# Log-sum-exp per head: batch 6's results are finished at the end of the kernel instead of at tiles 57 and 58

## The chip, the cores and the metric

The kernel runs on one core of a Trainium2 chip. Five engines work beside each other, each through its own list of instructions in order: TensorE (PE; its weight loads are listed as PEld), VectorE (DVE), ScalarE (ACT), GpSimd (POOL) and SyncE (SP), which here issues DMAs. A DMA can also be issued from ACT's list. The metric is the time on the device of one execution, in microseconds (us). Three timed runs of the kernel before gave 322.15, 322.24 and 322.38; the median is 322.24.

## The reference

The input x has 8 batches of 2048 rows of 2048 float32 numbers. Each row is cut into 8 heads of 256, and each head has a bias of 256 numbers.

```python
x_heads = x.reshape(B, S, H, Dh).transpose(0, 2, 1, 3)
x_heads = x_heads + bias[None, :, None, :]
x_tiled = np.repeat(x_heads, 2, axis=2)
mx = x_tiled.max(axis=-1, keepdims=True)
lse = mx.squeeze(-1) + np.log(np.exp(x_tiled - mx).sum(axis=-1))
```

So for each batch, head and row the output is the logarithm of the sum of exp(x + bias) over the head's 256 numbers, written twice in succession. The output has the shape 8 x 8 x 4096.

## The kernel before

A tile is 256 rows: 128 partitions with 2 rows (`K = 2`) of 2048 numbers each. There are 64 tiles, 8 to a batch; the program calls the count `T` and numbers the tiles 0 to 63. Eight tile buffers (`xb`) are filled by DMAs from SP. All of x is read once, 134 MB.

The kernel takes no maximum. For each head of each row it needs the sum of exp(x + bias). Some heads have their bias added in PSUM by TensorE (two multiplications, one that lays down the bias and one that adds x through the identity), and ACT takes the exponential and the sum in one instruction (L458 in the last tiles, followed by an instruction that reads the accumulator). For the others ACT takes the exponential of x alone (L483), and DVE multiplies by exp(bias) and sums (L518, `weigh`), or POOL multiplies and folds in halves (L535, L541) and DVE sums the remaining 32 (L548). In most tiles (0 to 53) POOL adds the bias ahead of the exponential (L477) and DVE sums (L502). The sums go to small tiles `R`, one for each group of batches.

The last three tiles, 61 to 63, are not worked on as tiles. The text `TAIL` lists, word by word, which step is put into the program next: an addition in PSUM (`add`, L806), an exponential (`exp`), a sum with bias (`sum`), a weighing, a fold. The rows of these tiles are called e, f, a, b, c and d; "b:0" is head 0 of row b. Their loads are cut into 13 pieces, `TAIL_LOADS`, in the order in which they are wanted; the last three are c:01, b:0 and b:1. The list ends with the sum of b:0 (ACT) and the sum of the folded c:7 (DVE). Both belong to batch 7.

The whole program is in an order written out by hand: each engine runs its instructions in the order in which the program calls them. Waits between engines follow from the tiles that instructions read and write. An instruction that the scheduler would tie to another bank of the same PSUM tile is freed from it by `on_bank`. PSUM has two tiles of two banks each, `pairs`; banks 0 and 1 are the first pair, 2 and 3 the second. A counter, `n_ps`, hands out the banks in turn. It goes up by 1 for each of the tiles 0 to 53, by 2 for each of the tiles 54 to 60 (one for each row), by 1 for each of the 11 words `add`, and by 1 in `turn_two`.

When the sums of some batches are complete they are turned by TensorE, so that rows lie along the free dimension, ACT takes the logarithm and writes each number twice, and a DMA stores the result. There are four such endings:

- two groups of batches 0 to 5, in `finish` (L577), at tiles in the middle, into `res`;
- batch 6, in `turn_two` (L698, two turns of 128 x 64) and `finish_two` (L711, 64 x 512 out), into `res_two`;
- batch 7, in `finish_last` (turn L716, logarithm L722, DMA L723 issued from ACT), into `res_last`, as the last thing.

In the kernel before, `turn_two` is called at the end of tile 57 (`t == T - 7`) and `finish_two` at the end of tile 58. The stores of the first two groups and of batch 6 are all issued in `store`, which is called ahead of the list of the last tiles. On SP they stand behind the last loads, in this order: L582 twice, L586 once.

Last of all `judge` looks at the bit patterns of the sums (L607, L626, L633): when an exponential was out of range, a slow second version would compute everything again. Every engine reads this verdict and branches. Then SP waits for every DMA, the stores among them, and the kernel ends.

Of the kernel before, what the change touches and what calls it, by code (L numbers as in the profile page):

```python
# [92 lines left out]
def kernel(  # L93
# [6 lines left out]
    nc = tc.nc  # L100
    P = nc.NUM_PARTITIONS
    B, S, D = x.shape
    H, Dh = bias.shape
    assert D == H * Dh and S % (P * KB) == 0
    NBLK = S // (P * K)
    NB = S // (P * KB)
    TB = KB // K
    T = B * NBLK
# [55 lines left out]
    res_two = sb.tile([H * NBLK, P, K, 2], F32, name="res_two")  # L164
# [12 lines left out]
    def modes_of(t):  # L177
        return [modes for t0, modes in STAGES if t0 <= t][-1]

    def pieces(t):  # L180

        if len(modes_of(t)) == 1:
            return [(0, K, 0, D)]
        return [(k, k + 1, 0, D) for k in range(K)]
# [85 lines left out]
    for set_idx, (_name, funcs) in enumerate(get_activation_tables(nc.m.arch).items()):  # L270
# [9 lines left out]
        out=brow.rearrange("p (h j) -> p h j", h=H), in_=bias.unsqueeze(0)  # L280
# [25 lines left out]
    for i, c in enumerate(range(G0, D, MM)):  # L306
# [10 lines left out]
        out=b_far,  # L317
        in_=brow,
# [5 lines left out]
        out=Rx[0][0:1, 1 + widths[0] :],  # L324
# [11 lines left out]
    def other_factors():  # L336
        nc.scalar.activation(
            out=w_ps[:, W_LATE - W0 :], in_=b_rep[:, W_LATE - G0 : W2 - G0], func=ACT.Exp
        )
        nc.scalar.activation(out=w_sb, in_=b_rep[:, W1 - G0 :], func=ACT.Exp)  # L340
# [7 lines left out]
    def on_bank(i, ins):  # L348
        for j, u in bank_users[i // 2]:
            if j != i and u.ins.engine != ins.ins.engine:  # L350
                tc.declare_no_dep(ins.ins, u.ins, reason="another bank")
        bank_users[i // 2].append((i, ins))
        return ins
# [68 lines left out]
    def late_heads(m, t, got, sums):  # L422


        mms = []
        for h, p in enumerate(got[:-1]):
            mm = nc.tensor.matmul(  # L427
                p,
                lhsT=ident,
                rhs=xts[t % NBUF][:, :, h * Dh : (h + 1) * Dh],  # L430
                start=False,
                stop=True,
            )
            mms.append(on_x(t, mm, [loads[t, 0, 0]]))

        def pe_part():
            for k in range(K):
                act = nc.scalar.activation(  # L438
                    out=xts[t % NBUF][:, k, 0:Dh],
                    in_=got[0][:, k * Dh : (k + 1) * Dh],  # L440
                    func=ACT.Exp,
                    accum_out=sums[:, k, 0:1],
                )
                last_uses[t].append(on_x(t, act, [mms[0]]))
            act = nc.scalar.activation(  # L445
                out=xts[t % NBUF][:, :, Dh : m["pe"] * Dh].rearrange(
                    "p k (h j) -> p h k j", j=Dh
                ),
                in_=got[-1].rearrange("p (h k j) -> p h k j", k=K, j=Dh),
                func=ACT.Exp,  # L450
            )
            on_x(t, act, [mms[-1]])

        return pe_part
# [124 lines left out]
    def store():  # L579

        for (b0, b1), r in zip(groups, res):
            nc.sync.dma_start(  # L582
                out=out[b0:b1].rearrange("b h (n r) -> (b h n) r", n=NB),
                in_=r.rearrange("q p k r -> q (p k r)"),
            )
        nc.sync.dma_start(  # L586
            out=out[B - 2].rearrange("h (n r) -> (h n) r", n=NBLK),
            in_=res_two.rearrange("q p k r -> q (p k r)"),
        )

    def ends_of(i):

# [100 lines left out]
    def turn_two():  # L693
        bank = n_ps[0] % len(ps)
        n_ps[0] += 1
        two_in.append(bank)
        for k in range(K):
            turn = nc.tensor.transpose(  # L698
                out=ps[bank][0 : H * NBLK, k * P : (k + 1) * P],
                in_=R[B - 2][:, k].rearrange("p h n -> p (h n)"),  # L700
                identity=ident,
            )
            on_bank(bank, turn)

    def finish_two():
        (bank,) = two_in
        two = ps[bank][0 : H * NBLK]
        tv = bass.AP(
            tensor=two.tensor, offset=two.offset, ap=[two.ap[0], [1, P], [P, K], [0, 2]]
        )  # L710
        on_bank(bank, nc.scalar.activation(out=res_two, in_=tv, func=ACT.Ln))  # L711

    def finish_last():
        bank = n_ps[0] % len(ps)
        last = ps[bank][:, 0:P]
        nc.tensor.transpose(  # L716
            out=last, in_=R_last.rearrange("p h n k -> p (h n k)"), identity=ident
        )
        tv = bass.AP(
            tensor=last.tensor, offset=last.offset, ap=[last.ap[0], [1, P], [0, 2]]  # L720
        )
        nc.scalar.activation(out=res_last, in_=tv, func=ACT.Ln)  # L722
        nc.scalar.dma_start(  # L723
            out=out[B - 1].rearrange("h (n r) -> (h n) r", r=2 * P),
            in_=res_last.rearrange("q p r -> q (p r)"),
        )


    def sums_of(t):

        b, blk = divmod(t, NBLK)
        if b < B - 2:
            return R[b][:, blk % TB * K :, :, blk // TB]
        if b == B - 2:
            return R[b][:, :, :, blk]
        return R_last[:, :, blk, :].rearrange("p h k -> p k h")
# [107 lines left out]
    for t in range(T_TAIL):  # L844
        if t == T_FACTORS:
            other_factors()
        xt = xts[t % NBUF]
        sums = sums_of(t)
        for k0, k1, c0, c1 in pieces(t):
            m = modes_of(t)[k0]  # L850
            add = None
            heads = []
            bias_here = bias_there
            if m["late"]:
                pe_part = late_heads(m, t, bias_here, sums)
                if t == BLOCKS - TB - 1:
                    keep_warm()
            else:
                heads = add_x(m, t, k0, c0, c1, bias_here)

                pe_parts = [
                    lambda t=t, one=one, sums=sums: sum_biased(t, *one, sums)
                    for one in heads
                ]

                def pe_part(pe_parts=pe_parts):
                    flush(pe_parts)

            if not m["late"]:
                if next_units:  # L870
                    bias_there = put_bias(*next_units.pop(0))
            if t > T_PROMPT and m["g0"] == H:
                keep_warm()
            if m["g0"] < H:
                add = g_add(m, t, k0, k1)
            wait_for_pool = t == T_ROWS and k0 == 0
            if not wait_for_pool:
                flush(for_pool)
            h0 = m["pe"]
            h1 = m["g0"]  # L880
            hf = min(h1, H - m["fold"])
            if h0 < h1 and not m["late"]:
                done = exp_inplace(
                    t, xt[:, k0:k1, h0 * Dh : h1 * Dh], loads[t, k0, c0]
                )
                if wait_for_pool:
                    flush(for_pool)
                if hf < h1:
                    for_pool.append(fold(t, k0, hf, h1, sums, [done]))
            flush(for_pe)  # L890
            if not m["late"]:
                for k in range(k0, k1):
                    for h in range(h0, hf):
                        weigh(
                            t,
                            xt[:, k, h * Dh : (h + 1) * Dh],
                            h,
                            sums[:, k, h : h + 1],
                            done,
                        )  # L900

            def pool_part(t=t, m=m, k0=k0, k1=k1, sums=sums, add=add):
                if add:
                    later(m, t, k0, k1, sums, add)
                if k1 == K:
                    reload(t)

            for_pool.append(pool_part)
            if m["g0"] < H:
                pe_part()  # L910
                if t == T_PROMPT - 1:
                    first_factors()
                if m["late"]:
                    bias_there = put_bias(*next_units.pop(0))
                    if t == BLOCKS - TB - 1:
                        keep_warm()
            else:
                for_pe.extend(pe_parts)

        for i, (_, b1) in enumerate(groups):  # L920
            if t - 2 == b1 * NBLK - 1:
                finish(i)
                ends_of(i)
        if t == T - 7:
            turn_two()
        if t == T - 6:
            finish_two()
    store()
    last_bank = heads[0][2]
    to_read[last_bank] = len(for_pe)  # L930
# [6 lines left out]
    for what, row, heads, step in tail:  # L937
# [7 lines left out]
            tail_step(what, *row, heads, step)  # L945
        next_bias()
    assert not for_pe and not for_pool and not to_bias
    finish_last()
    again = judge() > 0

# [33 lines left out]
```

## Time and profile before

| | |
|---|---|
| median of the timed runs | 322.24 us |
| the profiled execution, its own time | 322.7 us |
| its span (first to last instruction) | 320.8 us |
| busy: PE, DVE, ACT, POOL | 77%, 89%, 82%, 90% of the span |
| mean DMA rate | 422 GB/s |
| mean granted TensorE clock | 0.948 |

The profile page gives for each engine its busy time, then groups of instructions by source line ("L711"), and the chain of work that ended last: from the last instruction back to what released it, and so on. A row of a group reads: line, engine, operation, tile written <- tile read, partitions x elements, and the count or the time. A timeline gives the start and the duration of each instruction, and in brackets how long its engine stood idle before it and what it waited for. For a DMA it gives the time that the issuing took; the time to landing, from the issue to the last arrival, stands in the list of DMAs. Times in the views are counted from the start of the span, so the end is at 320.8.

### The profile page before, as it was taken

Reading aid. Unit: us, or ns where it says so; the run is one execution under the profiler, and the core shown is the slowest. Engines: PE = TensorE matmul, PEld = TensorE weight load, DVE = VectorE, ACT = ScalarE, POOL = GpSimd, SP = SyncE. Lnnn points to the kernel's source line nnn. Section 1 sums busy time; section 2 is a strip of 40 time slices with the busy share of each in tenths; the row PEclk is TensorE's granted clock in tenths of the full one; section 3 lists DMA queues with packets and bytes.
Section 4 is the critical chain, followed back from the end, with each engine's and each line's share of the span. In section 5 each row is a group of like instructions: output and inputs, shape, how many; then the busy total and the mean of one; then the engine's idle time right before and its main releaser. Section 6 shows DMA issues by size and latency. Waiting matters only on the chain.

```text
span 320.8 us, 2284 instructions
## 1 busy us (share of the span) xinstructions
PE 248.0 (77%) x619; PEld 100.3 (31%) x619; DVE 286.6 (89%) x303; ACT 263.7 (82%) x437; POOL 287.4 (90%) x116
## 2 busy tenths in 40 slices
PE   5998884977886679868677778877877788597774
PEld 1333332323332224323223323332332332143332
DVE  1337999699989998998999998999999999989996
ACT  1149987698698877879889879888888998999996
POOL 7949997999999999999999999999999999976874
PEclk9989997899799997979999979999999999779998
DMA  7999999999999999999999999999999999999995
GB/s 295 462 421 458 392 459 443 404 453 441 413 453 400 450 447 404 449 441 414 453 410 441 449 402 453 413 435 427 425 435 434 433 425 426 426 428 425 424 413 205
DMA packets 8950, 135.44 MB, mean 422 GB/s; under 512 B 996, under 2 KB 1511, under 8 KB 2791
## 3 DMA queue, kind: packets, MB, share of 16 engines
q1 hardware_dynamic: 8784, 135.14, 98.5%
q10 hardware_dynamic: 152, 0.14, 0.1%
q8 instruction: 5, 0.08, 0.1%
q14 instruction: 9, 0.07, 0.1%
HBM read 134.23 MB, written 1.05 MB: 422 GB/s over the span
## 4 chain that ended last, share of the span: by engine, by line
DMA 42%; DVE 28%; ACT 13%; PE 9%; POOL 6%; issue 0%; SPq 0%
DMA xb<-in_x_dram 42%; DVE R L502 22%; ACT xb L483 10%; POOL xb L477 6%; DVE xb L495 4%; PE pair L427 3%; ACT xb L458 3%; DVE xb L518 2%; PE one_ps L427 2%; PE pair L302 1%; PE pair L369 1%; PE pair L404 1%; DMA brow<-in_bias_dram 1%; ACT xb L445 1%; PE one_ps L369 1%
## 5 line engine op out<-in xcount | busy, mean ns | idle before, releaser
L477 POOL TENSOR_TENSOR xb<-xb,b_rep 128x2048 f32<-128x2048 f32 x57 | 257.6, 4544 | 18.9 <-DMA xb<-in_x_dram 18.9
L502 DVE TENSOR_REDUCE R<-xb 128x14 f32<-128x3584 f32 (+1 forms) x57 | 216.8, 3804 | 3.1 <-ACT xb L483 1.3
L483 ACT ACTIVATE xb<-xb 128x2560 f32<-128x2560 f32 (+8 forms) x79 | 156.7, 1995 | 19.5 <-POOL xb L477 19.5
L427 PE MATMUL pair<-xb,ident 128*128 128x512 f32 x216 | 110.5, 637 | 0.0
L427 PE MATMUL one_ps<-xb,ident 128*128 128x512 f32 x108 | 61.8, 655 | 17.0 <-DMA xb<-in_x_dram 17.0
L445 ACT ACTIVATE xb<-pair 128x1024 f32<-128x1024 f32 x54 | 55.4, 1026 | 17.4 <-PE pair L427 17.1
L427 PEld LDWEIGHTS pair<-xb,ident 128*128 128x128 f32 x216 | 44.3, 205 | 57.8 <-issue 57.8
L495 DVE TENSOR_TENSOR xb<-xb,w_ps 128x512 f32<-128x512 f32 x54 | 36.7, 680 | 20.8 <-ACT xb L483 20.8
L369 PE MATMUL one_ps<-b,ones_bf 128*128 128x512 bf16 x52 | 20.1, 387 | 37.3 <-ACT xb L438 37.3
L438 ACT ACTIVATE xb<-one_ps 128x256 f32<-128x256 f32 x108 | 39.8, 376 | 7.0 <-PE one_ps L427 7.0
L369 PEld LDWEIGHTS <-ones_bf 128*128 128x128 bf16 (+1 forms) x174 | 17.6, 101 | 86.2 <-issue 79.2
L369 PE MATMUL pair<-b,ones_bf 128*128 128x512 bf16 x104 | 30.9, 379 | 0.0
L427 PEld LDWEIGHTS one_ps<-xb,ident 128*128 128x128 f32 x108 | 19.5, 198 | 32.1 <-DMA xb<-in_x_dram 26.2
L518 DVE CUSTOM_DVE_ANT_0 xb<-xb,w_ps 128x256 f32<-128x256 f32 x60 | 22.1, 417 | 0.0
L438 ACT ACTIVATION_READ_ACCUMULATOR xb<-one_ps 128x1 f32 x108 | 22.0, 204 | 0.0
L404 PE MATMUL pair<-xb,ident 128*128 128x512 f32 x28 | 16.6, 698 | 4.9 <-DMA xb<-in_x_dram 4.9
L541 POOL TENSOR_TENSOR xb<-xb 128x128 f32<-128x128 f32 (+3 forms) x36 | 14.0, 388 | 3.3 <-ACT xb L817 0.5
L458 ACT ACTIVATE xb<-pair 128x256 f32<-128x256 f32 x39 | 15.1, 410 | 0.3 <-PE pair L404 0.3
L535 POOL TENSOR_TENSOR xb<-xb,w_sb 128x256 f32<-128x256 f32 (+1 forms) x11 | 9.1, 830 | 4.9 <-ACT xb L483 4.4
L806 PE MATMUL pair<-xb,ident 128*128 128x256 f32 (+1 forms) x22 | 8.1, 456 | 3.4 <-DMA xb<-in_x_dram 3.2
L418 PE MATMUL tp<-b_rep,ident 128*128 128x384 f32 x24 | 9.7, 485 | 0.0
L458 ACT ACTIVATION_READ_ACCUMULATOR xb<-pair 128x1 f32 x39 | 9.3, 238 | 0.0
(59 smaller groups left out, 82.2 us busy)
## 6 DMA issues: line engine op xcount, KB each, us to landing
xb<-in_x_dram SPq DMA_DIRECT2D x20, 4096.0 KB, 21.9
xb<-in_x_dram SPq DMA_DIRECT2D x17, 2048.0 KB, 22.3
xb<-in_x_dram SPq DMA_DIRECT2D x10, 1024.0 KB, 22.3
xb<-in_x_dram SPq DMA_DIRECT2D x2, 640.0 KB, 18.1
xb<-in_x_dram SPq DMA_DIRECT2D x3, 384.0 KB, 12.3
xb<-in_x_dram SPq DMA_DIRECT2D x1, 768.0 KB
xb<-in_x_dram SPq DMA_DIRECT2D x2, 256.0 KB, 15.4
out_dram<-res SPq DMA_DIRECT2D x1, 512.0 KB, 5.8
```

The lines of the kernel that those rows point to most:

```text
L369: nc.tensor.matmul(p, lhsT=lhsT, rhs=each_row(b, h * Dh, Dh, K), start=i == 0, stop=False,)
L404: mm = nc.tensor.matmul(p, lhsT=ident, rhs=xts[t % NBUF][:, ka:kb, c : c + w], start=False, stop=True,)
L427: mm = nc.tensor.matmul(p, lhsT=ident, rhs=xts[t % NBUF][:, :, h * Dh : (h + 1) * Dh], start=False, stop=True,)
L438: act = nc.scalar.activation(out=xts[t % NBUF][:, k, 0:Dh], in_=got[0][:, k * Dh : (k + 1) * Dh], func=ACT.Exp, accum_out=sums[:, k, 0:1],)
L445: act = nc.scalar.activation(out=xts[t % NBUF][:, :, Dh : m["pe"] * Dh].rearrange("p k (h j) -> p h k j", j=Dh), in_=got[-1].rearrange("p ...
L458: act = nc.scalar.activation(out=xts[t % NBUF][:, k, h * Dh : (h + 1) * Dh], in_=p, func=ACT.Exp, accum_out=sums[:, k, h : h + 1],)
L477: add = nc.gpsimd.tensor_tensor(out=v, in0=v, in1=each_row(b_rep, c - G0, D - c, k1 - k0), op=ALU.add)
L483: return on_x(t, nc.scalar.activation(out=v, in_=v, func=ACT.Exp), [after])
L495: mul = nc.vector.tensor_tensor(out=f, in0=f, in1=each_row(w_ps, m["pe"] * Dh - W0, n, k1 - k0), op=ALU.mult,)
L502: red = nc.vector.tensor_reduce(out=sums[:, k0:k1, h0:H], in_=v.rearrange("p k (h j) -> p k h j", j=Dh), op=ALU.add, axis=mybir.AxisListTy ...
L518: ttr = nc.vector.tensor_tensor_reduce(out=v, in0=v, in1=w, scale=1.0, scalar=0.0, op0=ALU.mult, op1=ALU.add, accum_out=dst,)
L541: done = nc.gpsimd.tensor_tensor(out=v[:, :, 0:n], in0=v[:, :, 0:n], in1=v[:, :, n : 2 * n], op=ALU.add)
```

## The change

Batch 6's turn, logarithm and store are all called behind the list of the last tiles, ahead of `finish_last`. TensorE's two turns come behind the addition of b:0, ACT's logarithm behind the sum of b:0. The DMA that stores `res_two` moves from `store` to `finish_two`; it is still SP's third store and last DMA. The bank counter no longer goes up between tiles 57 and 58.

```diff
@@ store
-        nc.sync.dma_start(
-            out=out[B - 2].rearrange("h (n r) -> (h n) r", n=NBLK),
-            in_=res_two.rearrange("q p k r -> q (p k r)"),
-        )
@@ finish_two
         on_bank(bank, nc.scalar.activation(out=res_two, in_=tv, func=ACT.Ln))
+        nc.sync.dma_start(
+            out=out[B - 2].rearrange("h (n r) -> (h n) r", n=NBLK),
+            in_=res_two.rearrange("q p k r -> q (p k r)"),
+        )
@@ the loop over the tiles
-        if t == T - 7:
-            turn_two()
-        if t == T - 6:
-            finish_two()
     store()
@@ behind the list
     assert not for_pe and not for_pool and not to_bias
+    turn_two()
+    finish_two()
     finish_last()
     again = judge() > 0
```

## The prediction

> **What bounds the kernel now.** I read the page first, then busy time by stage, the chain that ended last, ScalarE's own timeline, and the DMA issues. All numbers are microseconds from the span's start unless said otherwise. First the page and the stages of the last 37 us; a stage's row gives its length, busy time of PE, weight loads, DVE, ACT and POOL, granted clock, DMA share and GB/s.
>
> ```profile
> span 320.8 us, 2284 instructions
> core 0: us, PE busy (x) PEld busy (x) DVE busy (x) ACT busy (x) POOL busy (x), PEclk, DMA share, GB/s
> 294.70:305.70 11.00, 8.32 (x25) 3.60 (x24) 10.63 (x66) 11.00 (x27) 8.36 (x20) 1.00 1.01 424
> 305.70:310.70 5.00, 4.23 (x15) 2.06 (x16) 4.91 (x27) 5.00 (x14) 4.04 (x5) 1.00 1.01 414
> 310.70:317.40 6.70, 4.29 (x17) 2.07 (x16) 6.63 (x40) 6.67 (x23) 5.01 (x11) 1.00 0.91 351
> 317.40:320.83 3.43, 0.54 (x4) 0.26 (x4) 0.46 (x2) 0.38 (x1) 0.00 (x0) 0.64 0.13 44
> ```
>
> From 294.7 to 317.4 ScalarE is busy 11.00 of 11.00, 5.00 of 5.00 and 6.67 of 6.70: it has no gap. The DMA engines are full too until the loads run out. So two things run side by side here, and the question is which is ahead. The chain that ended last answers it.
>
> ```profile
> 294.18 0.73 ACT xb L458 x4
> 294.91 0.45 ACT res_two L711
> 295.36 1.37 ACT xb L483
> ...
> 309.79 0.96 ACT xb L483
> 310.74 0.02 issue
> 310.77 0.42 DVE xb L518
> ...
> 317.16 0.10 DVE R L548
> 317.26 0.15 DVE odd L607
> 317.41 0.01 issue
> 317.42 0.33 PE pair L716
> ```
>
> The chain runs on ScalarE and then on VectorE, and batch 6's logarithm (L711) is a link of it. The operation to be moved stands on the path that sets the end. The hand-over to DVE at 310.77 is close: ACT's last sum ends later still, as its timeline shows (columns: start, duration, engine, line, operation, and in brackets idle time before it).
>
> ```profile
> 294.66 0.25 ACT L458 ACTIVATION_READ_ACCUMULATOR xb<-pair 128x1 f32 x1
> 294.75 0.60 ACT L711 ACTIVATE res_two<-pair 64x512 f32<-64x512 f32 x1
> 295.23 1.50 ACT L483 ACTIVATE xb<-xb 128x1536 f32<-128x1536 f32 x1
> ...
> 316.15 0.49 ACT L483 ACTIVATE xb<-xb 128x256 f32<-128x256 f32 x1
> ...
> 316.82 0.46 ACT L458 ACTIVATE xb<-pair 128x256 f32<-128x256 f32 x1
> 317.08 0.29 ACT L458 ACTIVATION_READ_ACCUMULATOR xb<-pair 128x1 f32 x1
> 317.79 0.38 ACT L722 ACTIVATE res_last<-pair 128x256 f32<-128x256 f32 x1 [0.42 <-PE pair L716]
> 318.20 0.39 ACTq L723 DMA_DIRECT2D out_dram<-res_last  x1
> ```
>
> The last sum of the list (b:0) ends at 317.08 + 0.29 = 317.37. Batch 7's turn (L716) starts at 317.42, its logarithm at 317.79, its store at 318.20. DVE's last result is there at 317.26, 0.11 earlier. So ACT is the later of the two by a hair. Behind its last sum ACT stands idle for 0.42 while TensorE turns batch 7.
>
> **The change, part by part.** The sum is made against the profiled execution, 322.7 (a span of 320.8 and 1.9 around it); the median of the three timed runs is 322.24, 0.46 lower, and I carry the difference over to it.
>
> *The logarithm out of tile 58's place.* L711 lasts 0.60, but its successor starts 295.23 - 294.75 = 0.48 behind it, and the chain puts it at 0.45. I take 0.45. No instruction on ACT behind it waits for anything until 317.37, so all of them can start 0.45 earlier if their inputs are there. That needs three covers.
>
> *Cover 1, the loads.* The last loads are issued as those ahead of them land, behind any buffer that ACT still holds. The first two rows are the issue of the load before the last and its time to landing, the third is TensorE's addition of b:0.
>
> ```profile
> L242 SPq DMA_DIRECT2D xb<-in_x_dram x1: 328/328/328, 308.9 to 308.9; - x1
> DMA to landing us min/median/max: 6.3/6.3/6.3
> 315.62 0.60 PE L806 MATMUL pair<-xb,ident 128*128 128x256 f32 x2
> ```
>
> The load before the last is issued at 308.9 and lands at 315.2. The last one (b:1, 128 KB) follows it; at the 424 GB/s of the stage that is 0.31 more, 315.5 (an estimate from these rows). Its exponential starts at 316.15, and would start at 315.70. It still has about 0.2. TensorE adds b:0 in the two multiplications that end at 315.62 + 0.60 = 316.22; its sum starts at 316.82, and would start at 316.37, with 0.15 left. So the loads allow a gain of about 0.45 + 0.15 = 0.6 and no more: the gain is capped just above what I claim.
>
> *Cover 2, DVE.* It must move with ACT, since L716 needs its sums too.
>
> ```profile
> 305.70 0.42 DVE L518 CUSTOM_DVE_ANT_0 xb<-xb,one_ps 128x256 f32<-128x256 f32 x1 [0.38 <-ACT xb L483]
> ```
>
> At 305.70 DVE has been idle for 0.38, waiting for an exponential. At 310.77 the chain hands over from ACT to DVE, so DVE waits for ACT there as well. I count the 0.38 alone: its end goes to 317.26 - 0.38 = 316.88, still before ACT's 317.37 - 0.45 = 316.92, so ACT's 0.45 decides.
>
> *The two turns out of tile 57, into the end.* These are two weight loads and two multiplications on TensorE.
>
> ```profile
> 288.05 0.38 PE L698 MATMUL pair<-ident,R 128*64 128x128 f32 x2
> 317.42 0.33 PE L716 MATMUL pair<-ident,R 128*128 128x128 f32 x1 [1.20 <-DVE odd L607]
> ```
>
> At tile 57 they take 0.38 on an engine that waits for loads there, so removing them gives 0. At the end they are queued behind b:0's addition and ahead of L716. TensorE idles 1.20 before L716, and batch 6's sums were complete many tiles ago, so the 0.38 fits: 0. They need a PSUM bank. Counting the bank counter through the program (68 units of bias, 11 additions), they get bank 3, in the second pair, last read by d:0's sum, which is done before 315.2. Batch 7's turn gets bank 0, in the first pair, as before. So L716 does not wait for batch 6's logarithm. All additions from tile 58's second row on use the bank one lower; the distance between two uses of a bank stays four or grows by one. ACT waits for no addition in that stretch, so that is 0.
>
> *The logarithm into the end.* Queued on ACT behind b:0's sum and ahead of L722. Its place costs 0.48; ACT's free place there is 317.79 - 317.08 less the 0.09 by which L711 starts behind such a read (294.66 to 294.75), that is 0.62. It fits with 0.14 to spare, and moves as a whole with b:0's sum. If the cover were gone, L722 and all behind it would be late by the excess, at most 0.48. I take 0.
>
> *The store.* SP issues it in both kernels as its last DMA, so no load and no store is queued behind it; only SP's read of the verdict and its closing waits are, and the verdict comes later than the issue ends. Before, it was issued early:
>
> ```profile
> 313.05 0.47 SPq L586 DMA_DIRECT2D out_dram<-res_two  x1
> out_dram<-res SPq DMA_DIRECT2D x1, 512.0 KB, 5.8
> out_dram<-res SPq DMA_DIRECT2D x1, 256.0 KB, 5.4
> L582 SPq DMA_DIRECT2D out_dram<-res x2: 343/446/549, 311.1 to 312.1; - x2
> out_dram<-res_two SPq DMA_DIRECT2D x1, 128.0 KB, 4.8
> out_dram<-res_last ACTq DMA_DIRECT2D x1, 128.0 KB, 1.8
> ```
>
> It landed at 317.85, while batch 7's store lands at 318.20 + 1.8 = 320.0 and the span ends 0.8 later. In the new place batch 6's logarithm ends at 316.72 + 0.60 = 317.32 and the store is issued at about 317.35, 0.4 ahead of batch 7's (318.20 - 0.45 = 317.75). The end does not move if it takes less than 317.75 + 1.8 - 317.35 = 2.2. No row shows an SP store into an idle queue. Its bounds are 1.8 (L723, as many bytes, queues empty) and 4.8 (its own row, issued behind 768 KB of stores and the last loads: 512 and 256 KB). The last of those stores lands at 312.1 + 5.4 = 317.5, about when the new issue is made, so hardly anything stands ahead of it. I take 1.8, which costs 0.
>
> [...]
>
> The sum: -0.45 + 0 + 0 + 0 = -0.45. That is 322.25 for a profiled execution and 321.79 for the median, 0.14% less.
>
> **The rivals.** 0.2% is 0.64 us, about what a measurement of this kernel can tell from no change.
>
> 1. *Batch 6's store becomes the last thing to land* (slower). It is exposed where before it had 2 us of cover. At 4.8 it lands at 322.15 instead of batch 7's 320.0 before: +2.15, 324.4. From 2.65 on the change is a loss, from 3.3 on a loss over 0.2%. For it: no row shows the short case on SP. Against it: nothing is left in the queue ahead of it.
> 2. *The loads take the gain.* In the timed runs the loads may land later against ACT than in this execution; 0.6 of later landing eats all of it: 322.24. For it: DMA share 1.01 and only 0.15 to spare. Against it: ACT has no wait in the whole stretch.
> 3. *The end is not covered on ACT or TensorE*: L716 or L722 waits for batch 6's logarithm after all. L716 would start at 317.32 rather than 316.97: +0.35, net -0.10, 322.14. Against it are the banks counted above.
> 4. *The two stores collide.* If batch 7's 128 KB queue wholly behind batch 6's, at 424 GB/s, the end is 0.31 later: net -0.14, 322.1. Against it: the issues are 0.4 apart and each needs 0.31. [...]
> 5. *More than the sum.* If the logarithm's whole 0.60 and the 0.1 or so by which DVE's and TensorE's starts are loosened came back, it would be -0.7, 321.54. Against it: the cap of 0.6 from the loads.
>
> **How the numbers follow.** The forecast (321.79, itself between 321.6 and 321.95) has 0.60; rival 1 has 0.09, rival 2 0.12, rival 3 0.05, rival 4 0.04, rival 5 0.10. Rivals 2, 3 and 4 and the forecast lie within 0.2%. Rival 5 is faster by over 0.2% for the most part, and a little of the forecast's tail with it: 0.13. Rival 1 is slower by over 0.2% for the larger part: 0.08. The rest, 0.79, is no change. The range of 321.45 to 322.55 takes in the forecast, rivals 2 to 5 and the mild end of rival 1, and leaves its 4.8 out.
>
> **What would show it.** In the profile after: an L483 row directly behind the sums of tile 58, with no L711; every ACT start from there on 0.4 to 0.5 earlier; L716 near 316.97; L711's row between b:0's read and L722, with L722's idle time gone or down to about 0.1; a store of 128 KB from SP landing 1.8 to 2.2 after issue. Wrong would be: ACT waiting for a load or an addition behind 295 (rival 2), L716 waiting for res_two's line (rival 3), the SP store at 2.65 or more (rival 1), or L723 above 1.8 (rival 4).

## The result and the profile after

The change made the kernel slower: 323.00 us against 322.28 (medians of 13 runs each), a ratio of 1.0020 with a 95% interval of 1.0011 to 1.0028. That is 0.72 us. The forecast was 0.45 us less than before.

The profiled execution took 322.93, with a span of 321.1. First the end of the list on ScalarE, TensorE and SP after the change, from the timeline (start, duration, engine, line, operation, idle time before it).

```profile
316.36 0.39 ACT L458 ACTIVATE xb<-pair 128x256 f32<-128x256 f32 x1
316.63 0.21 ACT L458 ACTIVATION_READ_ACCUMULATOR xb<-pair 128x1 f32 x1
316.72 0.59 ACT L707 ACTIVATE res_two<-pair 64x512 f32<-64x512 f32 x1
317.26 0.38 ACT L722 ACTIVATE res_last<-pair 128x256 f32<-128x256 f32 x1
317.68 0.39 ACTq L723 DMA_DIRECT2D out_dram<-res_last  x1
...
316.08 0.38 PE L694 MATMUL pair<-ident,R 128*64 128x128 f32 x2
316.90 0.33 PE L716 MATMUL pair<-ident,R 128*128 128x128 f32 x1 [0.43 <-DVE odd L603]
...
317.33 0.47 SPq L708 DMA_DIRECT2D out_dram<-res_two  x1
```

On ScalarE and TensorE the end looks as the prediction drew it. Batch 6's logarithm (now L707) fills the gap behind the last sum, L722 starts with no idle time before it, and batch 7's turn starts at 316.90, near the 316.97 foretold. That last agreement is luck: in a second execution of the kernel before, shown below, the turn starts at 317.00 without the change. The loss comes behind the turn. The list of DMA issues (bytes, and us from issue to landing) shows where:

```profile
out_dram<-res_two SPq DMA_DIRECT2D x1, 128.0 KB, 2.6
out_dram<-res_last ACTq DMA_DIRECT2D x1, 128.0 KB, 2.6
```

Batch 7's store took 1.8 before; now both stores of 128 KB take 2.6. Batch 7's, issued at 317.68, lands at 320.3 instead of 320.0, and the span ends 0.8 behind it, as before.

That explains 0.3 of later landing, and 0.3 of longer span, but not the 0.72 between the medians. The rest is in the profile that the prediction read, as the first experiment shows.

### The profile page after: what moved, and what is told of

Same layout as the page of the kernel before. It is cut to its first block, busy times and chain, and to the rows that moved or that the text cites. A ratio compares the mean times of both kernels' runs of the same rounds, so it can differ in the third digit from the quotient of the medians.

```text
span 321.1 us, 2283 instructions
## 1 busy us (share of the span) xinstructions
PE 247.9 (77%) x618; PEld 100.6 (31%) x619; DVE 286.6 (89%) x303; ACT 264.5 (82%) x437; POOL 287.5 (90%) x116
## 3 DMA queue, kind: packets, MB, share of 16 engines
HBM read 134.23 MB, written 1.05 MB: 421 GB/s over the span
## 4 chain that ended last, share of the span: by engine, by line
DMA 42%; ACT 19%; POOL 17%; DVE 11%; PE 10%; issue 0%; SPq 0%
DMA xb<-in_x_dram 41%; POOL xb L477 17%; ACT xb L483 13%; DVE R L502 8%; PE pair L427 4%; ACT xb L458 3%; PE one_ps L427 2%; ACT xb L445 2%; DVE xb L495 1%; PE pair L302 1%; PE pair L369 1%; ACT xb L438 1%; PE one_ps L369 1%; DMA brow<-in_bias_dram 0%; DVE xb L518 0%; DVE R L593 0%
## 5 line engine op out<-in xcount | busy, mean ns | idle before, releaser
L427 PEld LDWEIGHTS pair<-xb,ident 128*128 128x128 f32 x216 | 45.0, 208 | 58.4 <-issue 58.4
L404 PEld LDWEIGHTS pair<-xb,ident 128*128 128x128 f32 x28 | 4.9, 197 | 14.7 <-DMA xb<-in_x_dram 12.9
```

Source lines behind the costliest of these rows:

```text
L404: mm = nc.tensor.matmul(p, lhsT=ident, rhs=xts[t % NBUF][:, ka:kb, c : c + w], start=False, stop=True,)
L427: mm = nc.tensor.matmul(p, lhsT=ident, rhs=xts[t % NBUF][:, :, h * Dh : (h + 1) * Dh], start=False, stop=True,)
```

## Experiments

### The kernel before, profiled again

> The kernel before, profiled once more. Theory G (the profile that the prediction read was a late execution, because the granted clock was 0.50 from 282 to 284 where tile 56 was added): the span is near 320.4 and the sum of tile 56 that began at 284.60 begins near 284.2, unless the clock is low at the same place again. Rival (the profile was a usual one, and the kernel after loses elsewhere): the span is 320.8 again with the clock near 1.0 from 282 to 284.

The time was 322.18 (one run), the span 320.4: 0.4 shorter than in the profile that the prediction read. Of 21 timed runs of the kernel before, taken beside it, the median is 322.26 and the highest 322.79, so this execution is a usual one and the 322.7 of the first was near the upper end. ScalarE's timelines of the two executions part in one place. Here are the granted clock by stage, TensorE's additions for tile 56 and the sum on ScalarE that waits for them. First the profile that the prediction read (in the stages the last three columns are clock, DMA share, GB/s):

```profile
278.00:280.00 2.00, 1.57 (x3) 0.15 (x1) 2.00 (x8) 2.00 (x9) 2.00 (x1) 0.50 1.00 422
280.00:282.00 2.00, 0.99 (x1) 0.50 (x2) 2.00 (x3) 1.51 (x3) 1.66 (x2) 0.50 1.04 438
...
281.01 3.55 PE L404 MATMUL pair<-xb,ident 128*128 128x512 f32 x4 [1.44 <-DMA xb<-in_x_dram]
...
284.60 0.38 ACT L458 ACTIVATE xb<-pair 128x256 f32<-128x256 f32 x1 [0.28 <-PE pair L404]
```

Then the second execution of the same kernel:

```profile
278.00:280.00 2.00, 0.52 (x3) 0.02 (x1) 2.00 (x6) 2.00 (x8) 2.00 (x1) 1.00 1.03 434
280.00:282.00 2.00, 1.02 (x2) 0.49 (x3) 2.00 (x5) 1.69 (x4) 1.67 (x2) 0.92 0.99 418
...
280.98 3.11 PE L404 MATMUL pair<-xb,ident 128*128 128x512 f32 x4 [2.46 <-DMA xb<-in_x_dram]
...
284.18 0.38 ACT L458 ACTIVATE xb<-pair 128x256 f32<-128x256 f32 x1
...
316.44 0.41 ACT L458 ACTIVATE xb<-pair 128x256 f32<-128x256 f32 x1
...
317.36 0.38 ACT L722 ACTIVATE res_last<-pair 128x256 f32<-128x256 f32 x1 [0.42 <-PE pair L716]
317.78 0.39 ACTq L723 DMA_DIRECT2D out_dram<-res_last  x1
```

In the first execution the clock stood at 0.50 from 278 to 284; in the second at 1.00, then 0.92, and at 0.50 only from 282 on. The loads of tile 56 landed at 281 in both. The four multiplications took 3.55 and 3.11, and the sum behind them started at 284.60, having waited, and at 284.18, without waiting. The difference of 0.42 was kept to the end: the last sum (b:0) starts at 316.82 there and at 316.44 here, L722 at 317.79 and 317.36. The expectation placed the low clock at 282 to 284, where it is 0.50 in both; what differs is the time ahead of that. All ten traces of this case have the same work up to tile 57. In the other nine these four multiplications took 1.98 (in the run with the late store, clock 1.00 throughout) to 3.11, and the sum behind them did not wait. Only in the profile that the prediction read was the clock at 0.50 all the way from 278 to 284, and only there did it wait. The clock was not varied on its own. That the execution was 0.4 late, and from 284.6 on, is shown.

So in a usual execution ScalarE stands 0.4 earlier. The loads behind it do not: TensorE's weight load for the second row of tile 60 starts at 300.87, and at 300.70 in the profile that the prediction read. ScalarE's exponential of that row starts 0.2 behind it (301.06), where it stood 0.8 behind (301.49). So 0.6 of the room that the prediction gave the loads is not there.

### After, without batch 6's store

```diff
@@ finish_two
-        nc.sync.dma_start(
-            out=out[B - 2].rearrange("h (n r) -> (h n) r", n=NBLK),
-            in_=res_two.rearrange("q p k r -> q (p k r)"),
-        )
```

> The kernel after without the DMA that stores batch 6 (its rows of the output are not written); turn and logarithm stay at the end. Theory C+L (the end is late because two stores are in flight at once, and the loads had taken most of the gain on ScalarE): batch 7's store is back at 1.8, and the time is 0.1 to 0.2 below that of before, near 322.1. The prediction's sum with only the store mispriced: 0.45 below before, near 321.8. If the loss lies in the turns or the logarithm at the end: 322.9 to 323.0, as the kernel after.

Measured: 322.28 against 322.26 for before, ratio 1.0000 (0.9991 to 1.0009). Without the store the whole loss is gone. A gain at tile 58 and an equal cost at the end would leave the same time, so the timeline has to decide. Here are ScalarE's exponentials of tile 60's second row and of row f, each followed by TensorE's weight load that waits for the same load, and then the end on ScalarE:

```profile
300.90 1.49 ACT L483 ACTIVATE xb<-xb 128x1536 f32<-128x1536 f32 x1 [0.20 <-DMA xb<-in_x_dram]
300.92 0.30 PEld L404 LDWEIGHTS pair<-xb,ident 128*128 128x128 f32 x2 [1.07 <-DMA xb<-in_x_dram]
...
305.76 1.27 ACT L483 ACTIVATE xb<-xb 128x1280 f32<-128x1280 f32 x1
305.78 0.30 PEld L802 LDWEIGHTS pair<-xb,ident 128*128 128x128 f32 x2 [1.49 <-DMA xb<-in_x_dram]
...
316.49 0.39 ACT L458 ACTIVATE xb<-pair 128x256 f32<-128x256 f32 x1
317.38 0.38 ACT L718 ACTIVATE res_last<-pair 128x256 f32<-128x256 f32 x1
```

From the start of b:0's sum to batch 7's logarithm it is 0.89 here and 0.92 in the second execution of before (316.44 to 317.36), so the turns and batch 6's logarithm cost nothing at the end. And b:0's sum starts no earlier than there, so taking 0.47 off ScalarE's list at tile 58 gained nothing.

ScalarE, ahead of its place by the missing logarithm, waits for the load of tile 60's second row and starts at 300.90, together with TensorE's weight load. In the second execution of before it was 0.2 behind that load. It catches up with the load of row f too, at 305.76 and 305.78. No idle time is listed there, since the instruction before it ends only at 305.79; in the second execution of before the two start at 305.80 and 305.72. The lead is 0.16 at the first of these exponentials and 0.04 at the second. The kernel after shows the same: 300.73 and 300.75 for tile 60, 305.59 and 305.61 for row f. The loads have taken the gain whole.

### Before, with the logarithm twice

```diff
@@ finish_two
         on_bank(bank, nc.scalar.activation(out=res_two, in_=tv, func=ACT.Ln))
+        on_bank(bank, nc.scalar.activation(out=res_two, in_=tv, func=ACT.Ln))
```

> The kernel before with batch 6's logarithm written twice at tile 58. Theory L (ScalarE's list and the loads are even there; taking the logarithm out gave nothing because the loads then held ScalarE): adding 0.48 is not held back by anything, and costs 0.35 to 0.48, so 322.6 to 322.75. Rival (ScalarE has slack in a usual execution, and the profile that the prediction read misled on that): less than 0.1, so 322.3.

Measured: 323.06 against 322.39, ratio 1.0026 (1.0016 to 1.0036), 0.67 more. The place it takes on ScalarE:

```profile
294.36 0.61 ACT L711 ACTIVATE res_two<-pair 64x512 f32<-64x512 f32 x1
295.00 0.59 ACT L712 ACTIVATE res_two<-pair 64x512 f32<-64x512 f32 x1
...
317.10 0.43 ACT L458 ACTIVATE xb<-pair 128x256 f32<-128x256 f32 x1
```

The second logarithm starts 295.00 - 294.36 = 0.64 behind the first, so the edit adds 0.64 and not 0.48. Both write the same tile; whether that is the reason was not tested. All of it arrives at the end: b:0's sum moves from 316.44 to 317.10. So the work added to ScalarE cost its full price here (0.67 for 0.64), and the 0.47 removed paid nothing: within the 0.1 to 0.2 seen above, the list and the loads are even there. The theory's direction holds; its size was low, since it took the second logarithm to start as soon behind the first as other instructions do.

### One store alone at the end, in four combinations

The kernel after issues a store of 64 partitions with 2 KB each from SP, and one of 128 partitions with 1 KB each from ScalarE. Both are 128 KB. Three runs, each with one of the two stores removed (its rows of the output are not written), tell apart whether the company, the queue or the shape makes them slow. The fourth combination, batch 7's alone from ScalarE, is the run without batch 6's store above. Batch 6's alone, from SP:

```diff
@@ finish_last
-        nc.scalar.dma_start(
-            out=out[B - 1].rearrange("h (n r) -> (h n) r", r=2 * P),
-            in_=res_last.rearrange("q p r -> q (p r)"),
-        )
```

> The kernel after without the DMA that stores batch 7 (its rows of the output are not written). Theory C (the two stores hold each other up): batch 6's store, alone now, lands 1.8 after its issue, and the span is near 320.0. Theory S (a store of 64 partitions with 2 KB each is slow by itself, whatever is beside it): it lands 2.4 to 2.6 after its issue, as in the kernel after, and the span is near 320.8.

Batch 7's alone, from SP (batch 6's DMA removed as above):

```diff
@@ finish_last
-        nc.scalar.dma_start(
+        nc.sync.dma_start(
             out=out[B - 1].rearrange("h (n r) -> (h n) r", r=2 * P),
```

> The kernel after without batch 6's store, and with batch 7's store (128 partitions of 1 KB) issued from SP instead of from ScalarE. Alone at the end, batch 6's store took 2.24 from SP, batch 7's takes 1.76 from ScalarE. Theory Q (the queue of SP costs the difference): 2.2 here. Theory P (64 partitions of 2 KB cost it): 1.8 here.

Batch 6's alone, from ScalarE (batch 7's DMA removed as above):

```diff
@@ finish_two
-        nc.sync.dma_start(
+        nc.scalar.dma_start(
             out=out[B - 2].rearrange("h (n r) -> (h n) r", n=NBLK),
```

> The kernel after without batch 7's store, and with batch 6's store (64 partitions of 2 KB) issued from ScalarE instead of from SP. Theory Q (the queue of SP): 1.8 to landing. Theory P (64 partitions of 2 KB): 2.2 to landing, and ScalarE's read of the verdict, 0.49 long where SP has the store, takes about 1.05, as SP's did there.

The rows of the DMA lists, in the order of these three runs, and with each the read of the verdict by the engine that issued the store (duration min/median/max in ns):

```profile
out_dram<-res_two SPq DMA_DIRECT2D x1, 128.0 KB, 2.2
L636 SPq TENSOR_LOAD <-verdict x1: 1052/1052/1052, 318.0 to 318.0; - x1
```

```profile
out_dram<-res_last SPq DMA_DIRECT2D x1, 128.0 KB, 1.7
L636 SPq TENSOR_LOAD <-verdict x1: 532/532/532, 318.0 to 318.0; - x1
```

```profile
out_dram<-res_two ACTq DMA_DIRECT2D x1, 128.0 KB, 2.3
L636 ACTq TENSOR_LOAD <-verdict x1: 984/984/984, 317.9 to 317.9; - x1
```

| store, alone at the end | from SP | from ScalarE |
|---|---|---|
| batch 6's: 64 partitions of 2 KB | 2.2 | 2.3 |
| batch 7's: 128 partitions of 1 KB | 1.7 | 1.8 (without batch 6's store) |

The queue makes no difference, the shape makes 0.5. Theory P holds against theory Q. Of the theories of the first of these runs neither holds alone: 2.2 lies between the 1.8 of theory C and the 2.4 to 2.6 of theory S. The shape takes batch 6's store from 1.8 to 2.2, and the company takes it from 2.2 to 2.6 and batch 7's from 1.8 to 2.6. Fewer partitions and longer rows were not told apart: both changed together, and no run shows why they cost 0.5.

The verdict rows show a second effect. The engine that issued the store of 64 partitions reads its verdict in about 1.0 instead of 0.5. SP's closing waits stand behind its read, and they end the kernel. Here are their rows (count, duration in ns, start of the first and of the last) in the second execution of before, with batch 6's store alone from SP, and in the kernel after:

```profile
L979 SPq EVENT_SEMAPHORE  x10: 17/28/28, 318.8 to 320.3; - x10
L973 SPq EVENT_SEMAPHORE  x10: 17/28/28, 319.5 to 320.8; - x10
L977 SPq EVENT_SEMAPHORE  x10: 17/28/28, 319.5 to 321.1; - x10
```

With batch 6's store alone from SP the time was 322.69 (one run) and the span 320.8, although the store landed at 317.43 + 2.2 = 319.6, about as early as batch 7's lands in the second execution of before (317.78 + 1.7 = 319.5, time 322.18, span 320.4). SP came to its waits 0.7 later there, and they then took 1.3, as they also did in the three other runs in which SP issued the last store. That the span is theory S's 320.8 is SP's doing and not the landing's. In the second execution of before the waits took 1.5, because one of them stood until the store had landed. With batch 6's store from ScalarE, landed at 319.6 too, SP read its verdict in 0.48, and the span was 320.5 (322.36, one run). With batch 7's alone from SP the time was 322.12 (one run).

So the late store of this shape from SP costs twice, in its landing (2.2 where batch 7's takes 1.7) and in SP's read (1.05 where it takes 0.53), and the two costs overlap. In the kernel after SP came to its waits at 319.5 as well; with 1.3 from there the span would be about 320.8, an estimate, 0.4 above 320.4, even if both stores had landed. Batch 7's store, which lands at 320.3, takes it on to 321.1.

### Both stores from one queue

```diff
@@ finish_last
-        nc.scalar.dma_start(
+        nc.sync.dma_start(
             out=out[B - 1].rearrange("h (n r) -> (h n) r", r=2 * P),
```

> The kernel after with batch 7's store issued from SP, behind batch 6's, instead of from ScalarE: one queue in place of two. If the loss comes from two queues in turn on the same DMA engines (theory C): batch 7's store lands near 320.0 or before, and the time is 0.3 or more below that of the kernel after. If it comes from batch 6's store being slow by itself (theory S): batch 7's waits for it in the queue all the same, and the time is that of the kernel after, 323.0, or up to 0.2 more because the issue on SP begins behind the first one.

Measured: 322.82 against 322.26, ratio 1.0017 (1.0008 to 1.0026). That overlaps the interval of the kernel after, so one queue or two can't be told apart in the time. The DMA rows and SP's issues:

```profile
out_dram<-res_two SPq DMA_DIRECT2D x1, 128.0 KB, 2.4
out_dram<-res_last SPq DMA_DIRECT2D x1, 128.0 KB, 2.1
...
317.37 0.47 SPq L708 DMA_DIRECT2D out_dram<-res_two  x1
317.94 0.53 SPq L723 DMA_DIRECT2D out_dram<-res_last  x1
```

Batch 7's store lands at 317.94 + 2.1 = 320.0, as early as theory C had it, but the time fell by 0.18 only and not by 0.3 or more. Here the landing does not end the kernel: SP, behind two issues and a read of 0.70, comes to its closing waits at 319.7, and they take 1.3, to 321.0. The pair costs about the same in one queue and in two. Both stores take longer than alone (2.2 to 2.3 and 1.7 to 1.8) either way, 2.6 and 2.6 from two issuers, 2.4 and 2.1 from one; no run shows which DMA engines carried them.

### Before, with only the store late

```diff
@@ store
-        nc.sync.dma_start(
-            out=out[B - 2].rearrange("h (n r) -> (h n) r", n=NBLK),
-            in_=res_two.rearrange("q p k r -> q (p k r)"),
-        )
@@ finish_last
-        nc.scalar.dma_start(
+        nc.sync.dma_start(
             out=out[B - 1].rearrange("h (n r) -> (h n) r", r=2 * P),
             in_=res_last.rearrange("q p r -> q (p r)"),
         )
+        nc.sync.dma_start(
+            out=out[B - 2].rearrange("h (n r) -> (h n) r", n=NBLK),
+            in_=res_two.rearrange("q p k r -> q (p k r)"),
+        )
```

> The kernel before, turn and logarithm of batch 6 at tiles 57 and 58 as there, but its store issued from SP behind batch 7's store, which is issued from SP too. If the late store is the whole loss of the kernel after (theory P): batch 7's store lands 1.8 to 1.9 after its issue at about 317.8, batch 6's is issued about 0.5 behind it and lands 2.2 to 2.4 later, near 320.6, and the time is 0.7 to 1.1 above before, with the logarithm where it was. If the late logarithm or the turns have a part in the loss: the time is clearly nearer to before than the kernel after is, less than 0.4 above it.

Measured: 323.46 against 322.24, ratio 1.0041 (1.0027 to 1.0055), 1.2 more.

```profile
out_dram<-res_last SPq DMA_DIRECT2D x1, 128.0 KB, 1.7
out_dram<-res_two SPq DMA_DIRECT2D x1, 128.0 KB, 2.5
...
317.75 0.35 SPq L719 DMA_DIRECT2D out_dram<-res_last  x1
318.15 0.47 SPq L723 DMA_DIRECT2D out_dram<-res_two  x1
```

With turn and logarithm where they were, a late store alone makes the kernel slower, by more than the change did. Here batch 6's store comes last and lands at 318.15 + 2.5 = 320.65; batch 7's, ahead of it, takes its usual 1.7. The loss is 0.1 above the upper end of the expectation. SP's read of its verdict, behind the second issue, took 1.05; SP came to its closing waits at 320.2, and they took 1.3, so its own list ends the kernel about as late as the landing does. Moving batch 7's store to SP, which this edit does as well, is not the loss: alone from SP it left the time at 322.12. Together with the run without batch 6's store this settles the cause both ways: late logarithm without the store, no loss; late store without the late logarithm, the loss.

No version came out of this that beats the kernel before. The loads hold the end of the list where it is with or without the logarithm in it, so 322.28, without batch 6's store, is as far as this change got.

## Why the prediction was wrong

The forecast was no change with 0.79, at 321.79 in a range of 321.45 to 322.55. The time lies at 323.00, 0.2% slower. Two of the sum's four terms were wrong: the gain of 0.45 was 0.0, and the store, put at 0, cost 0.7.

- *The logarithm out of tile 58, 0.45 gained*: the size of the place was right (0.48 and 0.47 by the starts in the two executions of before), the gain was not. Measured, 0.0 without batch 6's store. The step that failed is **cover 1, the loads**: that they allow a gain of about 0.6 was worked out from one execution that ran 0.4 late from 284.6 on. In a usual one ScalarE is only 0.2 behind the load of tile 60's second row and 0.1 behind that of row f, and the gain is gone at the end. This was rival 2, given 0.12 and priced at 0.6 of later landing; the 0.6 came, 0.4 of it from ScalarE being earlier. The clue lay in the text: the profiled execution was 0.46 above the median, and the difference was carried over as if it lay outside the stretch that the argument used.
- *Cover 2, DVE*: DVE was not the later one; batch 7's turn started at 316.90, right behind ScalarE's last sum (316.63 + 0.21 = 316.84). But there was no 0.45 to keep up with, so this step was hardly tried.
- *The turns into TensorE's gap, the banks, the logarithm into ScalarE's gap*: all right. L694 stands in the gap at 316.08, L716 waits for nothing of batch 6, and L722 follows at 317.26. Rival 3 did not happen.
- *The store, "I take 1.8"*: the second **step that failed**, and the larger one. 1.8 was the row of a store of 128 partitions; batch 6's, of 64, takes 2.2 to 2.3 alone and 2.6 beside the other. The prediction took the nearest row by bytes and by the empty queue, and left the shape out.
- *The store, SP's verdict and closing waits*: the prediction named them as what stands behind the store and put them at nothing, since "the verdict comes later than the issue ends". The verdict was there at 317.71 and the issue ended at 317.80, and then the read took 1.08 instead of the 0.48 of before. By the run with batch 6's store alone this is worth about 0.4 by itself.
- *Rival 4, the two stores collide*: it was given 0.04 and priced at 0.31. Batch 7's store got 2.6 instead of 1.8, 0.8 later. It was priced at the DMA rate of the loads, 0.31 for 128 KB, and that was too little.
- *Rival 1, batch 6's store lands last*: it does not; 317.33 + 2.6 = 319.9 is ahead of batch 7's 320.3. Beside it the other one takes 2.6 instead of 1.8. But the side, an exposed store at the end as what makes it slower, was right.

The sum as measured, against the second execution of before: batch 7's store is issued 0.1 earlier (317.68 for 317.78) and takes 0.9 longer (2.6 for 1.7), 0.8 in all from rounded rows; the spans differ by 0.7 and the medians by 0.72.

## What to carry to other kernels

Here a saturated engine and the loads ran neck and neck, 0.1 to 0.2 apart: 0.47 taken off the engine gained 0.0, and 0.64 added to it cost 0.67. So measure the engine's lead over the loads before pricing a gain on it, in an execution at the median, and if the profiled one is not there, find the place where it fell behind before using its gaps. The small store moved to the very end made this kernel 0.72 slower: it took 2.6 to land, its neighbour took 2.6 instead of 1.8, and its issuer's next read took 1.08 instead of 0.48. Price such a store from a row of the same shape, not of the same size (2.2 to 2.3 and 1.7 to 1.8 for the same 128 KB), and ask what stands behind it in its issuer's list. In its old place it took 4.8 and still landed at 317.85, ahead of batch 7's at 320.0; finish work that needs a store where later work covers the landing so, even if, as here, it takes 0.47 of a busy engine.

## What the runs showed of the hardware

- Two stores of 128 KB, each alone at the end: 1.7 to 1.8 from 128 partitions with 1 KB each, 2.2 to 2.3 from 64 partitions with 2 KB each, from SP or from ScalarE.
- Two of them, one of each shape, issued 0.35 apart from two engines: 2.6 each, 0.4 and 0.8 more than alone.
- An engine whose last issue was the store of 64 partitions took 0.98 to 1.08 for its next read of one number into a register; engines that had issued no store at the end took 0.48 to 0.55. ScalarE, which had issued the other store in the kernel after, took 0.84. Why was not tested.
- The same kernel, twice profiled, differed by 0.4 in its span. In the longer one the granted clock was 0.50 from 278 to 284 and tile 56's four multiplications took 3.55; in the other nine traces they took 1.98 to 3.11.
